# Which engine makes the weights' low parts while the first attention runs

## The chip, the cores and the metric

One core of one Trainium2 chip runs the whole program in one launch. The metric is the device time of an execution in microseconds (us), the median of several; lower is better. The names in the views: PE is TensorE's matrix unit (PEld its weight loads), DVE is VectorE, ACT is ScalarE, POOL is GpSimd, SP is SyncE, whose work here is to issue DMAs. L119 is line 119 of the kernel before; in the changed kernel every line from 1920 on stands one to three lines further down.

## The reference

One decoder layer on a sequence of 1024 tokens of width 1024. What matters here:

```python
h = rms_norm(x, norm1_g); proj = h @ w_in            # 54 column tiles of 128
p_rwkv, p_sb, q_mem, gate_logits = split(proj)
y_a = rwkv7_branch(p_rwkv, ...)                      # delta-rule recurrence, 8 heads x 64
y_b = stick_breaking_branch(p_sb, ...)               # "the first attention", 8 heads x 64
y_m = memory_branch(q_mem, mem, ...)                 # cross-attention into 256 memory tokens
x = x + (sum_b sigmoid(G_b) * (branch_b @ W_br[b])) @ W_out
x = x + conv_ffn(x)
```

Everything is float32.

## The kernel before

**How a product is made.** A float32 product goes to TensorE as three products of rounded operands: each operand is split into a high part (rounded to the format `fp32r`) and a low part (what the rounding left). For weights, `load_w` issues the DMA of a 128x1024 tile `wr` on SP's queue, `split_raw` lets ScalarE copy it to the high part `wh` (line 80) and another engine subtract to get the low part `wl = wr - wh` (line 81). Then `mm3` makes `wh.xhi`, `wh.xlo` and `wl.xhi` on TensorE (all matrix products are recorded under line 119, all transposes under line 105). `wr`, `wh` and `wl` have two buffers each, so the DMA of the next tile but one waits until both splitting engines have read the raw tile.

**How the work is ordered.** The program is written as a main stream with a filler. `run` builds `items`, a list of generators, each the projection of one weight tile (the heads' r, k, v: `shift_item`; the attention's values: `sb_v`; its q and k: `sb_qk`; branch gates: `gate_item`; the memory's keys and values: `mem_kv`). `stream` starts an item, that is, splits its weights, when the item before it begins its products, so a low part is made one item ahead of its first use. `weave` advances the main stream (with priority) and takes filler steps from `pump` between its steps. Main streams in turn: `rwkv_prep` for the four head pairs p = 0 to 3, then `sb_attn`, then `mem_attn` and the recurrence. During `sb_attn` the pump also steps through `inverse`, a chain of 62 pairs of VectorE instructions (lines 554 and 556) that inverts triangular blocks. A scheduler lays the instructions of each engine in one fixed order. An engine works through its own order and waits, at an instruction's place, for what that instruction needs.

**What the steps of the prediction touch.**
- In `rwkv_prep`: `chain(h)` (lines 464 to 474) builds two tiles per half on VectorE, among them `bk` by four instructions of line 472; `gram` (lines 476 to 494) multiplies them on TensorE and VectorE masks the result (line 486); lines 519 and 520 make a tile that ScalarE's line 522 must wait for, since it overwrites `g`, which line 520 reads; line 523 sends `g` to DRAM on ScalarE's queue, and a later `bk` takes over that buffer.
- In `differ` (lines 751 to 760): four tiles `A` are loaded by SP (line 756) and subtracted from on VectorE (line 757).
- In `sb_attn`: for each unit `front` makes logits on TensorE and their sigmoid on ScalarE (line 933), `weigh` runs a scan over them on VectorE (line 939), `mid` transposes the result on TensorE (line 105) and copies it back (line 951).
- POOL's other work in that stretch: small powers (lines 427, 781), a scaling (line 498) and DMAs (line 544).

Of the kernel before, what the change touches and what calls it, by code (L numbers as in the profile page):

```python
# [11 lines left out]
F32 = mybir.dt.float32  # L12
# [3 lines left out]
ALU = mybir.AluOpType  # L16
# [33 lines left out]
class Trunk:  # L50
# [27 lines left out]

    def split_raw(self, raw, hi, lo, fix=lambda ins: ins, fix_hi=None):
        (fix_hi or fix)(self.nc.scalar.activation(hi, raw, AF.Copy))  # L80
        fix(self.nc.gpsimd.tensor_tensor(lo, raw, hi.bitcast(F32), ALU.subtract))  # L81
        return hi, lo

    def split_w(self, src, fix=lambda ins: ins, fix_hi=None):
# [1821 lines left out]
    def run(self):  # L1906
        nc, tc = self.nc, self.tc
        self.setup()
        sx, sw, sl, sr = ExitStack(), ExitStack(), ExitStack(), ExitStack()
        self.pool_x = sx.enter_context(tc.tile_pool(name="xp", bufs=1))  # L1910
        self.pool_a = sr.enter_context(tc.tile_pool(name="ap", bufs=1, side="right"))
        self.bufs_w = {"w4": 3, "A": 4, "qk": 8, "at": 7, "ys": 1, "it": 1}
        self.pc = [self.pool_a.tile([128, NC], F32, name=f"pc{p}") for p in range(4)]
        self.inst = self.pool_a.tile([128, 64, 64], F32, name="inst", tag="inst")
        self.stored, self.open_gates = set(), []
        drain = lambda g: [None for _ in g]
        chain = itertools.chain
        self.pool_w = sw.enter_context(tc.tile_pool(name="w1", bufs=1, side="right"))
        krv, qk, mq = ([[] for _ in range(4)] for _ in range(3))
        krv[0].append(self.startup())  # L1920
        self.pin = True
        marks, self.fresh = {"k0"}, []
        self.marks = marks
        items = [self.shift_item(i + p, krv[p], f"{n}{p}") for p in range(4) for n, i in (("k", 4), ("r", 0), ("v", 8)) if (p, n) != (0, "k")]
        items += self.sb_v()
        self.v = []
        zero = self.t4("ys", n=512)
        nc.vector.memset(zero[0:1], 0.0)
        nc.sync.dma_start(self.vsd[0:1], zero[0:1])
        inv = self.inverse()  # L1930
        gq = [(b, d) for b in (1, 0) for d in range(8)]
        gq[14:14] = [(2, 0), (2, 1)]
        self.stored = set(gq)
        gate = lambda hook={}: self.gate_item(*gq.pop(0), hook)
        mark = lambda name: lambda: marks.add(name)
        for p in range(4):
            kp, kss, qp, early, hooks = self.sb_qk(p, qk[p])
            items += [*([self.differ] if p == 0 else []), kp, gate({**early, 6: self.spread_last} if p == 0 else early), kss, qp, gate(hooks), mark(f"sb{p}")]
        prep, mss, mv, mk = self.mem_kv()
        mqi = [None] * 4  # L1940
        for h in range(4):
            mqi[h] = self.mem_q(h, mq[h], {2: mqi[h - 1][1], 4: mark(f"mq{h - 1}")} if h > 1 else {})
        items += [gate({0: prep}), gate(), gate({2: prep}), lambda: mss(0), mv[0], lambda: mss(1), *mv[1:], *mk, mqi[0][0], mark("kv")]
        items += [self.mem_kss, gate({1: mqi[0][1]}), self.mem_kbc, mqi[1][0], mark("mq0")]
        items += [mqi[2][0], mqi[3][0], gate({2: mqi[3][1], 4: mark("mq3")}), gate(), mark("mem")]
        ld1, hk1, br1 = self.branch(1, True)
        ld2, hk2, br2 = self.branch(2, False)
        items += [lambda: drain(inv), gate(), ld1, gate(hk1), mark("y1"), *br1, ld2, gate(hk2), *br2, gate()]
        assert not gq
        pace = [0]  # L1950

        def pumped():
            due = 0
            for _ in self.stream(items):
                due += pace[0]
                while due >= 10:
                    due -= 10
                    next(inv, None)
                yield

        pump = pumped()

        def need(name):
            while name not in marks:
                next(pump)

        for p in range(4):
            self.weave(self.rwkv_prep(p, krv[p], need), pump, 1.0)
        pace[0] = 7
        need("sb0")  # L1970
        self.weave(self.sb_attn(qk, need), pump, 1.03, 0)
        need("kv")
        pace[0] = 8
        self.tight = True
        self.weave(self.mem_attn(mq, need), pump, 1.6, 0)
        self.tight = False
        need("mem")
        st2 = self.stage2()
        next(st2)
        need("y1")  # L1980
        self.weave(st2, pump, 2.15, 0)
        self.weave(self.group_norm(), pump, 1, 0)
        drain(pump)
        self.close_gates()
        self.pin = False
        sx.close()
        self.pool_l = sl.enter_context(tc.tile_pool(name="l4", bufs=16))
        self.branch_last()
        sums = self.out_proj()
        self.pool_a.tile([128, 56], F32, name="pad_a")  # L1990
        sw.close()
        self.bufs_r = {"u": 3, "p1": 2}
        self.pool_r = sr.enter_context(tc.tile_pool(name="ff", bufs=2, side="right", reuse_waits="tile"))
        self.up_phase(*sums)
        self.pool_r.tile([128, 40], F32, name="pad_r", bufs=1)
        self.down_phase()
        sr.close()
        sl.close()
# [67 lines left out]
```

## Time and profile before

| | |
|---|---|
| median of 3 runs | 1788.75 us (1787.13 to 1789.0) |
| the profiled execution's own time | 1788.76 us |
| its span (first to last instruction) | 1787.0 us, so 1.76 us lie around it |
| granted TensorE clock | 0.999 |
| busy share of the span: PE, DVE, ACT, POOL | 99%, 66%, 48%, 44% |
| low parts made under line 81 that the change moves | 41, on POOL 107.5 us |

How to read the views: a row of the timeline has start, duration, engine, line, operation, what it writes and reads, and in brackets how long its engine stood idle before it and who ended that. A group row has the count, then busy time and mean duration, then the idle time before. In a table by stages each engine has its busy time and, in brackets, its instructions. Matmuls overlap in the pipeline, so their rows' durations are longer than the distance between their starts.

### The profile page before, as it was taken

Reading aid. Unit: us, or ns where it says so; the run is one execution under the profiler, and the core shown is the slowest. Engines: PE = TensorE matmul, PEld = TensorE weight load, DVE = VectorE, ACT = ScalarE, POOL = GpSimd, SP = SyncE. Lnnn points to the kernel's source line nnn. Section 1 sums busy time; section 2 is a strip of 40 time slices with the busy share of each in tenths; the row PEclk is TensorE's granted clock in tenths of the full one; section 3 lists DMA queues with packets and bytes.
Section 4 is the critical chain, followed back from the end, with each engine's and each line's share of the span. In section 5 each row is a group of like instructions: output and inputs, shape, how many; then the busy total and the mean of one; then the engine's idle time right before and its main releaser. Section 6 shows DMA issues by size and latency. Waiting matters only on the chain.

```text
span 1787.0 us, 27327 instructions
## 1 busy us (share of the span) xinstructions
PE 1771.8 (99%) x10479; PEld 1440.1 (81%) x10479; DVE 1181.5 (66%) x1604; ACT 865.3 (48%) x1566; POOL 792.5 (44%) x448
## 2 busy tenths in 40 slices
PE   9999999999999999999999999999999999999999
PEld 7777778888888888777777888878888888888887
DVE  5667774898988624234443962687767777795597
ACT  6544343656666635534444334544444445454343
POOL 3223352331231453122332542487677677545454
PEclk9999999999999999999999999999999999999999
DMA  5145565111112443568554553223323323386476
GB/s 210 60 161 182 179 224 163 51 54 57 54 57 77 127 120 95 212 226 282 201 190 177 203 186 110 103 99 103 111 89 99 119 90 121 126 317 220 146 239 209
DMA packets 122771, 261.28 MB, mean 146 GB/s; under 512 B 28681, under 2 KB 43657, under 8 KB 122514
## 3 DMA queue, kind: packets, MB, share of 16 engines
q1 hardware_dynamic: 85026, 193.83, 32.9%
q10 hardware_dynamic: 33840, 53.10, 8.1%
q0 software_dynamic: 3776, 12.62, 2.4%
q8 instruction: 82, 1.34, 0.3%
q14 instruction: 47, 0.39, 0.1%
HBM read 178.99 MB, written 80.48 MB: 145 GB/s over the span
## 4 chain that ended last, share of the span: by engine, by line
PE 81%; DVE 6%; POOL 2%; issue 1%; ACT 1%; DMA 1%; DVEq 0%; SPq 0%; POOLq 0%; ACTq 0%
PE mm L119 66%; PE g L119 12%; PE g L105 3%; DVE it L554 1%; DVE at L939 1%; DVE inst L556 1%; DMA A<-yd 1%; POOL wl L1486 0%; DVE gall L1571 0%; DMA scr<-at 0%; POOL hf L781 0%; DVE w L344 0%; POOL l L1486 0%; DVE w L834 0%; DVE qk L877 0%
## 5 line engine op out<-in xcount | busy, mean ns | idle before, releaser
L81 POOL TENSOR_TENSOR wl<-wr,wh 128x1024 fp32r<-128x1024 f32 (+2 forms) x78 | 197.1, 2527 | 468.0 <-ACT wh L80 465.0
L119 PE MATMUL mm<-xhi,wh 128*128 128x512 f32 x784 | 260.3, 413 | 0.5 <-DVE w L331 0.4
L119 PE MATMUL mm<-xlo,wh 128*128 128x512 f32 x784 | 243.6, 392 | 0.0
L119 PE MATMUL mm<-xhi,wl 128*128 128x512 f32 x784 | 242.5, 391 | 0.0
L119 PEld LDWEIGHTS mm<-xlo,wh 128*128 128x128 f32 x784 | 147.1, 188 | 33.3 <-DVE xlo L208 0.4
L119 PEld LDWEIGHTS mm<-xhi,wl 128*128 128x128 f32 x784 | 147.0, 188 | 33.1 <-POOL wl L81 0.7
L119 PEld LDWEIGHTS mm<-xhi,wh 128*128 128x128 f32 x784 | 136.7, 190 | 28.9 <-issue 6.1
L80 ACT ACTIVATE wh<-wr 128x1024 fp32r<-128x1024 f32 (+2 forms) x78 | 81.8, 1049 | 130.9 <-PE mm L119 100.1
L119 PE MATMUL mm<-dw,da 128*128 128x512 f32 x528 | 120.3, 389 | 0.0
L119 PE MATMUL mm<-BT,l 128*128 128x512 f32 x504 | 118.0, 389 | 1.4 <-POOL l L1486 1.4
L1775 POOL TENSOR_TENSOR dw<-draw,dw 128x512 fp32r<-128x512 f32 x55 | 82.6, 1511 | 75.7 <-ACT dw L1773 70.0
L119 PEld LDWEIGHTS mm<-dw,da 128*128 128x128 f32 x528 | 99.1, 188 | 20.6
L119 PEld LDWEIGHTS mm<-BT,l 128*128 128x128 f32 x504 | 94.5, 188 | 21.5 <-POOL l L1486 1.8
L119 PE MATMUL mm<-BT,wh 128*128 128x512 f32 x352 | 108.7, 389 | 0.9 <-DVE BT L1396 0.9
L119 PE MATMUL mm<-B,wh 128*128 128x512 f32 x352 | 108.8, 390 | 0.0
L939 DVE TENSOR_TENSOR_SCAN at<-at,nrt 128x128 f32<-128x128 f32 (+3 forms) x64 | 96.3, 1514 | 18.2 <-ACT at L933 18.0
L1774 DVE TENSOR_TENSOR da<-draw,da 128x512 fp32r<-128x512 f32 x77 | 64.2, 839 | 51.5 <-ACT da L1772 51.2
L1486 POOL TENSOR_TENSOR l<-it,l 128x1024 fp32r<-128x1024 f32 x21 | 50.9, 2422 | 90.2 <-ACT l L1483 90.1
L119 PE MATMUL g<-dw,da 128*128 128x512 f32 x396 | 90.2, 389 | 0.0
L119 PEld LDWEIGHTS g<-dw,da 128*128 128x128 f32 x396 | 74.3, 188 | 15.4
L1772 ACT ACTIVATE da<-draw 128x512 fp32r<-128x512 f32 x77 | 48.2, 628 | 78.5 <-PE mm L119 32.0
L834 DVE TENSOR_TENSOR w<-w,nrt 128x1024 f32<-128x1024 f32 x24 | 46.6, 1941 | 57.3 <-ACT w L833 46.4
(337 smaller groups left out, 3979.2 us busy)
## 6 DMA issues: line engine op xcount, KB each, us to landing
wr<-in_w_in_dram SPq DMA_DIRECT2D x48, 512.0 KB, 3.6
draw<-actd SPq DMA_DIRECT2D x77, 256.0 KB, 2.9
draw<-in_w_down_dram SPq DMA_DIRECT2D x55, 256.0 KB, 4.6
at<-scr SPq DMA_DIRECT2D x24, 512.0 KB, 6.0
wr<-in_w_up_dram SPq DMA_DIRECT2D x22, 512.0 KB, 3.5
actd<-gall ACTq DMA_DIRECT2D x44, 256.0 KB, 3.2
rw<-in_w_up_dram SPq DMA_DIRECT2D x20, 512.0 KB, 3.5
gsd<-w ACTq DMA_DIRECT2D x18, 512.0 KB, 3.0
```

Of the source, the lines that this page charges most:

```text
L80: (fix_hi or fix)(self.nc.scalar.activation(hi, raw, AF.Copy))
L81: fix(self.nc.gpsimd.tensor_tensor(lo, raw, hi.bitcast(F32), ALU.subtract))
L105: self.pinned(self.nc.tensor.transpose(out, in_, self.ident[:n, :n]))
L119: self.pinned(self.nc.tensor.matmul(*a, **k))
L554: self.pinned(nc.vector.tensor_tensor(tv, X[:, 0:s, s : s + 1].to_broadcast([128, s, n]), X[:, s : s + 1, s + 1 : 64].to_broadcast([128, s ...
L556: self.pinned(nc.vector.tensor_tensor(X[:, 0:s, s + 1 : 64], X[:, 0:s, s + 1 : 64], tv, ALU.add))
L834: fix(nc.vector.tensor_tensor(g, g, self.nrb, ALU.mult))
L939: self.pinned(nc.vector.tensor_tensor_scan(sn[:, :W][:, ::-1], sn[:, :W][:, ::-1], self.nrt[:, 1152 - W :][:, ::-1], 1.0, ALU.mult, ALU.max))
L1486: ins = nc.gpsimd.tensor_tensor(lo, src, hi.bitcast(F32), ALU.subtract)
L1772: self.pinned(nc.scalar.activation(A[:, 0], a, AF.Copy))
L1774: self.pinned(nc.vector.tensor_tensor(A[:, 1], a, A[:, 0].bitcast(F32), ALU.subtract))
L1775: nc.gpsimd.tensor_tensor(Wt[:, 1], w, Wt[:, 0].bitcast(F32), ALU.subtract)
```

## The change

A field `low` of the class names the engine that runs line 81. It is POOL at the start, VectorE from the end of the first head pair's preparation, and POOL again from the end of the first attention.

```diff
     def split_raw(self, raw, hi, lo, fix=lambda ins: ins, fix_hi=None):
         (fix_hi or fix)(self.nc.scalar.activation(hi, raw, AF.Copy))
-        fix(self.nc.gpsimd.tensor_tensor(lo, raw, hi.bitcast(F32), ALU.subtract))
+        fix(self.low.tensor_tensor(lo, raw, hi.bitcast(F32), ALU.subtract))
         return hi, lo
...
         krv, qk, mq = ([[] for _ in range(4)] for _ in range(3))
+        self.low = nc.gpsimd
         krv[0].append(self.startup())
...
         for p in range(4):
             self.weave(self.rwkv_prep(p, krv[p], need), pump, 1.0)
+            self.low = nc.vector
         pace[0] = 7
         need("sb0")
         self.weave(self.sb_attn(qk, need), pump, 1.03, 0)
+        self.low = nc.gpsimd
```

41 instructions of line 81 leave POOL's order and stand in VectorE's: those for `wl_1015` to `wl_5640`. The orders of TensorE and ScalarE stay as they were. Three places in VectorE's order are of use later.

The first is in the fourth head pair's preparation, VectorE's order, as the difference between before (-) and now (+). `qk_2131` is the second half's other tile, `at_1752` the tile of lines 519 and 520, `wl_2031` and `wl_2077` are low parts of the attention's value weights:

```order
+L81 TENSOR_TENSOR wl_2031<-wr_2028,wh_2030 128x1024
 L519 TENSOR_TENSOR at_1752<-g_2046,at_1752 128x512
 L519 TENSOR_TENSOR at_1752<-g_2049,at_1752 128x512
-L467 SCALAR_TENSOR_TENSOR qk_2131<-qk_1867,at_1512 128x8x63
 L520 SCALAR_TENSOR_TENSOR at_1752<-at_1752,params,qk_1924 128x1024
-L468 TENSOR_SCALAR qk_2131<-at_1512 128x8
+L81 TENSOR_TENSOR wl_2077<-wr_2074,wh_2076 128x1024
 L757 TENSOR_TENSOR A_2278<-A_2278,w_314_1960 128x1024
 L486 TENSOR_TENSOR at_2086<-g_2087,kon 128x4x128
 L486 TENSOR_TENSOR at_2086<-g_2088,kon 128x4x128
+L757 TENSOR_TENSOR A_2281<-A_2281,w_319_1995 128x1024
 L486 TENSOR_TENSOR at_2108<-g_2109,kon 128x4x128
```

Two low parts come in; the rows of lines 467 and 468 taken out here now stand just ahead of `wl_2031`; and the second of the four `A` tiles (`A_2281`), which stood behind the second half's `bk`, now stands ahead of two masks of line 486 and of that `bk`. SP's order has its DMA ahead of the DMA of line 521 and of one weight tile, where it stood behind both.

The second place is the end of that preparation, VectorE's order again; `A_2284` and `A_2287` are the last two `A` tiles, `it_2311` is the first step of `inverse`:

```order
 L486 TENSOR_TENSOR at_2222<-g_2224,kon 128x4x128
 L757 TENSOR_TENSOR A_2284<-A_2284,at_2220 128x1024
+L81 TENSOR_TENSOR wl_2294<-wr_2291,wh_2293 128x1024
 L757 TENSOR_TENSOR A_2287<-A_2287,at_2252 128x1024
 L554 TENSOR_TENSOR it_2311<-inst 128x62
```

`wl_2294`, the low part for the first item after the values, stood in POOL's order behind a DMA; it now stands in VectorE's behind `A_2284`.

The third place is in the attention, VectorE's order as a difference; `it_4033` and `inst` belong to `inverse`, `at_4035` is a unit's scan, `w_682_4029` a branch gate:

```order
 L834 TENSOR_TENSOR w_682_4029<-w_682_4029,nrt 128x1024
 L554 TENSOR_TENSOR it_4033<-inst 128x972
+L81 TENSOR_TENSOR wl_4043<-wr_4040,wh_4042 128x1024
 L556 TENSOR_TENSOR inst<-inst,it_4033 128x36x27
 L939 SCALAR_TENSOR_TENSOR at_4035<-at_4035,nrt 128x128
```

Nothing but the low part comes in. The 1024-column scan of line 939 before it, which the prediction speaks of, stands three rows above this piece; `wl_3853`, the low part ahead of that scan, comes in twelve rows above the scan in the same way. SP's DMAs of weight tiles wait for VectorE's low part in this stretch where they waited for POOL's.

## The prediction

> **What bounds the kernel now.** I read the page first, then a table by stages over the stretch in which low parts move (125 to 640 us), then TensorE's waits in it, and last the timelines around each wait.
>
> ```profile
> PE 1771.8 (99%) x10479; PEld 1440.1 (81%) x10479; DVE 1181.5 (66%) x1604; ACT 865.3 (48%) x1566; POOL 792.5 (44%) x448
> sum 515.00, PE 511.50 PEld 419.20 DVE 388.42 ACT 278.73 POOL 168.50; mean PE 170.50 PEld 139.73 DVE 129.47 ACT 92.91 POOL 56.17
> PE g L105 <- DVE at L939: 1.8, 2, 1.6
> PE g L119 <- DVE qk L472: 1.2, 2, 1.0
> PE g L105 <- DVE at L336: 0.4, 1, 0.4
> ```
>
> TensorE works 99% of the span, and in the stretch it is idle for 515 - 511.5 = 3.5 us. All of its waits there, 1.8 + 1.2 + 0.4 = 3.4 us, end with VectorE. Neither TensorE's order nor its instructions change, so 3.5 us, 0.2% of the time, is about the most that the change can take away, whatever it frees elsewhere. What it can add has no such cap. A difference under 0.2% (3.6 us) is about what a measurement of this kernel cannot tell from no change.
>
> **The price of a moved instruction.** The groups of line 81 on POOL, and of the nearest VectorE operation:
>
> ```profile
> L81 POOL TENSOR_TENSOR wl<-wr,wh 128x1024 fp32r<-128x1024 f32 x41 | 107.5, 2621 | 205.4 <-ACT wh L80 205.3
> L877 DVE TENSOR_TENSOR qk<-w,qk 64x1024 fp32r<-64x1024 f32 x6 | 7.3, 1216 | 1.2 <-ACT qk L875 1.1
> ```
>
> VectorE has no row of this form. Line 877 is the same subtraction on the same types and row length, on half the partitions, and takes 1216 ns; POOL's own 2621 ns is the far end. I take 1.2 us, the row of the same engine: 41 x 1.2 = 49 us more work for VectorE (at the far end 107).
>
> But POOL's low parts already cost VectorE time. Two instructions of VectorE beside a low part on POOL, each followed by one of its form alone, and the last such case:
>
> ```profile
> 446.92 2.73 POOL L81 TENSOR_TENSOR wl<-wr,wh 128x1024 fp32r<-128x1024 f32 x1 [13.80 <-ACT wh L80]
> 447.42 3.27 DVE L554 TENSOR_TENSOR it<-inst 128x990 f32<-128x990 f32 x1
> 433.58 1.18 DVE L554 TENSOR_TENSOR it<-inst 128x990 f32<-128x990 f32 x1
> 136.66 2.85 DVE L466 TENSOR_TENSOR qk<-at,qk 128x512 f32<-128x512 f32 x1
> 189.25 0.69 DVE L466 TENSOR_TENSOR qk<-at,qk 128x512 f32<-128x512 f32 x1
> 612.21 2.42 DVE L554 TENSOR_TENSOR it<-inst 128x180 f32<-128x180 f32 x1
> ```
>
> POOL's low part ends at 446.92 + 2.73 = 449.65, and the instruction that began beside it ends at 450.69, one time of its own (1.18) later: it stood for 2.1 us. Each VectorE row that ran beside a moved low part, set against the shortest row of its form, gives 34 rows longer by over 0.15 us, the first at 136.66 and the last at 612.21, by 62 us in all. So VectorE pays 49 us and gets 62 back: its busy time in the stretch falls by about 13 us (ends: 13 us less; 107 us more, if none comes back at the far price).
>
> **Where a low part is later.** POOL made each one nearly as soon as its high part was there. VectorE makes it when its order comes to it. For `wl_4043`, in the attention:
>
> ```profile
> 463.85 2.51 POOL L81 TENSOR_TENSOR wl<-wr,wh 128x1024 fp32r<-128x1024 f32 x1 [5.27 <-ACT wh L80]
> 472.08 1.17 DVE L554 TENSOR_TENSOR it<-inst 128x972 f32<-128x972 f32 x1
> 483.03 0.62 PE L119 MATMUL mm<-xhi,wl 128*128 128x512 f32 x2
> ```
>
> Its place is behind the second row, which ends at 473.25, so it ends near 474.5, 8 us later than on POOL; TensorE's first use is at 483.0, because an item's weights are split an item ahead. That cover, 8.5 us here, hides the delay at no cost; gone, the 8 us would be TensorE's. The next DMA into the tile's buffer waits for the low part too, and is due only two items on. Put beside their first use in this way, the other places in the attention have 6 us or more, those before it less; the two thinnest follow below.
>
> **The wait at 468 us: 1.6 us go.**
>
> ```profile
> 464.03 4.47 DVE L939 TENSOR_TENSOR_SCAN at<-at,nrt 128x1024 f32<-128x1024 f32 x1
> 423.60 2.29 DVE L939 TENSOR_TENSOR_SCAN at<-at,nrt 128x1024 f32<-128x1024 f32 x1 [1.53 <-ACT at L933]
> 468.65 1.06 PE L105 MATMUL g<-kon,at 128*128 128x128 f32 x8 [1.57 <-DVE at L939]
> ```
>
> The scan met the low part of 463.85 and took 4.47 us where another of its form took 2.29; TensorE stood 1.57 us. With the low part behind the scan, it ends by 464.0 + 2.3 = 466.3, and TensorE is free for it at 468.65 - 1.57 = 467.1. Ahead of it `wl_3853` adds 1.2 us, and the hold at 447.42 gives back 2.1. I take -1.6 (ends: 0 and -1.6; the other 0.2 of this row and the 0.4 at line 336, another -0.6, I leave for the lower end).
>
> **The wait at 263 us: 1.2 us go.**
>
> ```profile
> 242.70 2.35 DVE L468 TENSOR_SCALAR qk<-at 128x8 f32<-128x8 f32 x1
> 244.96 2.80 DVE L472 TENSOR_TENSOR qk<-qk,qk 64x512 f32<-64x512 f32 x4
> 248.32 0.39 PE L119 MATMUL mm<-wl,xhi 128*128 128x512 f32 x1
> 250.19 3.40 DVE L520 SCALAR_TENSOR_TENSOR at<-at,params,qk 128x1024 f32<-128x1024 f32 x1
> 253.52 0.16 DVE L468 TENSOR_SCALAR qk<-at 128x8 f32<-128x8 f32 x1
> 254.81 0.34 ACTq L523 DMA_DIRECT2D ggd<-qk  x1
> 261.19 2.81 DVE L472 TENSOR_TENSOR qk<-qk,qk 64x512 f32<-64x512 f32 x4 [3.39 <-DMA ggd<-qk]
> 263.43 0.46 PE L119 MATMUL g<-qk,qk 64*128 64x128 f32 x2 [0.96 <-DVE qk L472]
> 264.14 1.01 PE L119 MATMUL g<-qk,qk 64*128 64x128 f32 x13 [0.26 <-DVE qk L472]
> ```
>
> A chain: line 520 was held by a low part on POOL, ScalarE's line 522 waited for it, its DMA left at 254.81, landed when VectorE's `bk` began at 261.19, and TensorE stood 0.96 + 0.26 = 1.2 us. Now the tiny line 468 at 242.70 takes the 0.16 us that it takes at 253.52. `bk` of the first half then ends at 242.9 + 2.8 = 245.7; lines 467 and 468, moved up, add 0.7; `wl_2031` ends at 247.6, 0.7 us ahead of its first use at 248.32 (ends: no cost, or 1.4 us if `bk` cannot begin before 244.96). Lines 519 and 520 add 2.5: 250.1, which is 3.5 us sooner than 253.59, and the DMA with it, so `bk` can begin at 257.7. Is VectorE there? Behind line 520 stand `wl_2077`, `A_2278` and two masks (3.6 us, 253.7), then the moved `A_2281`. Its DMA is now behind a weight tile's, which waits for `wl_2031`:
>
> ```profile
> 246.10 0.67 SPq L76 DMA_DIRECT2D wr<-in_w_v_dram  x1
> 254.52 0.67 SPq L756 DMA_DIRECT2D A<-vsd  x1
> DMA to landing us min/median/max: 5.2/6.6/7.5
> ```
>
> It leaves at about 247.6 + 0.7 = 248.3 instead of 254.52 and lands, as the four `A` tiles did, 5.2 to 7.5 us later: 253.5 to 255.8. Subtraction, two masks and line 466 (1.2 + 1.2 + 0.6) bring VectorE to `bk` at 256.7 to 258.8, its 2.8 us end by 261.6, and TensorE is free for it at 263.43 - 0.96 = 262.5. Cover 0.9 us. I take -1.2 (ends: -1.2, and +3 by the third rival).
>
> **The wait that comes in, at 285 us: 1.0 us.**
>
> ```profile
> 276.07 4.04 SPq L756 DMA_DIRECT2D A<-vsd  x2
> 283.59 1.34 DVE L757 TENSOR_TENSOR A<-A,at 128x1024 f32<-128x1024 f32 x1 [14.31 <-DMA A<-vsd]
> 284.83 0.62 PE L119 MATMUL mm<-xhi,wl 128*128 128x512 f32 x2
> ```
>
> VectorE stands 14.31 us for the DMA of `A_2284`; before, that held up nothing that TensorE needed soon. Now `wl_2294` is queued behind it: 283.59 + 1.3 + 1.2 = 286.1, and TensorE needs it at 284.83, 1.3 us sooner. That DMA goes out when the values that TensorE makes have been stored, so when TensorE gains 1.2 us at 263, both ends shift together. With its landing at the median of 6.6 in place of 276.07 to 283.59 = 7.5 us, 0.4 is left. I take +1.0 (ends: 0 and +1.3), nearer to the row of this very DMA.
>
> **The sum.** From the profiled execution's own 1788.76 us, which is the median of the runs (1788.75): -1.6 - 1.2 + 1.0 = -1.8, so 1787.0 us. Its own range is 1786.0 (nothing new at 285) to 1788.4 (1.4 late at 248). After 640 us nothing is moved, and TensorE's later work follows it.
>
> **The rivals.**
>
> *VectorE becomes the bound: slower.* Its slices in the attention are full:
>
> ```profile
> 380.00:400.00 20.00, 20.00 (x147) 17.11 (x145) 19.73 (x15) 12.76 (x25) 8.47 (x3) 1.00 0.15 44
> 400.00:420.00 20.00, 20.00 (x150) 16.56 (x149) 19.90 (x17) 10.75 (x21) 2.41 (x1) 1.00 0.17 60
> 440.00:460.00 20.00, 20.00 (x146) 16.56 (x144) 19.80 (x17) 15.96 (x28) 7.32 (x3) 1.00 0.14 40
> 460.00:480.00 20.00, 18.43 (x132) 15.53 (x130) 19.83 (x16) 9.30 (x18) 2.51 (x1) 1.00 0.09 27
> ```
>
> Each gets one low part. If nothing comes back, they need 79.26 + 4 x 1.2 = 84.1 of their 80 us, so the scans of line 939 reach TensorE up to 4.1 us later; both waits stay, and the one at 285 comes in: +5.1, 1793.9 us. It decides at the scan at 464: whether it takes 2.3 us or still 4.5. Against it speak the 34 held rows. The Trainium skill (Perfetto Trace Analysis, Optimizing Scalar/DVE Operations) says that work of a saturated VectorE may sensibly go to other engines, even GpSimd, which is the reverse of this change; by that rule the time would come out here. The same section warns that the two share a port into SBUF, so that moving work between them might not help; the held rows side with the warning. Chance 0.11.
>
> *All of TensorE's waits on VectorE go and none comes in.* Then -3.4: 1785.4 us; with the rest of the idle 3.5, 1785.2. For it: VectorE gets 13 us lighter, SP's queue ahead of the `A` tiles moves up too. Against it: the DMA at 276.07 waits for TensorE's own values. Chance 0.19.
>
> *The moved `A_2281` lands late.* If its DMA still leaves near 254.5 and lands at 261.9, `bk` ends 1.2 + 1.2 + 0.6 + 2.8 later, 267.7 instead of 264.0: TensorE loses 3.7 there in place of gaining 1.2, with -1.6 and +1.0 it is +3.1, 1791.9 us. For it: in that stretch many DMAs are under way. Against it: nothing in its new place waits past 248. Chance 0.07.
>
> *The time is only passed on.* TensorE gets ahead and stands the same 2.8 us at its next need of another engine, the sigmoids of line 933 say, as VectorE did before its scan at 423.60 (1.53 us). Then 0, 1788.8 us. Chance 0.15. That the change does not do what it says is ruled out by the order: 41 of line 81 stand in VectorE's.
>
> **How the numbers follow.** The forecast's case has what is left, 0.48. The range from 1785.0 to 1791.9 leaves out the slower rival and a little beyond the cap of 3.5 us. Faster by over 0.2% is below 1785.2: a part of the second rival, 0.13. Slower by over 0.2% is above 1792.3: the first rival and the tail of the third, 0.13. Within it: 0.74.
>
> **What would show it.** Right: in the profile after, VectorE's busy time from 125 to 640 us near 375 (388.42 - 13) with low parts of 1.2 us each; the scan at 464 at 2.3 us and no wait of TensorE behind it; `bk` near 258 and no wait at 263; a wait of about 1 us for a low part near 284. Wrong: VectorE's busy time at 430 or more, low parts of over 2 us, waits of TensorE on line 939 in the attention, or any wait of TensorE on a low part other than the one at 284, which would mean that a place in VectorE's order comes later than I read it.

## The result and the profile after

| | before | after |
|---|---|---|
| median (lowest to highest) of 19 runs each | 1788.23 us (1786.24 to 1790.78) | 1784.27 us (1783.01 to 1785.68) |
| ratio of after to before, 95% interval | | 0.9979 (0.9973 to 0.9985) |
| the profiled execution's own time; its span | 1788.76 us; 1787.0 us | 1783.84 us; 1782.1 us |

The changed kernel is 1788.23 - 1784.27 = 4.0 us faster, 0.21%. The forecast was 1787.0 us with a range from 1785.0: the direction was right, the gain larger than the range allowed.

The engines' line of the page; the row of the stretch from 125 to 640 us in the table by stages (PE, PEld, DVE, ACT and POOL in this order, then the granted clock, the DMA engines' busy share and their GB/s); all of TensorE's waits in that stretch (us in total, times, the longest); and the moved instructions by line, with duration in ns (least, median, most):

```profile
PE 1767.9 (99%) x10479; PEld 1438.4 (81%) x10479; DVE 1169.8 (66%) x1645; ACT 864.9 (49%) x1566; POOL 685.4 (38%) x407
```
```profile
125.00:640.00 515.00, 513.88 (x3467) 422.12 (x3466) 378.40 (x415) 279.07 (x477) 66.33 (x34) 1.00 0.35 111
```
```profile
PE mm L119 <- DVE wl L81: 0.8, 1, 0.8
PE g L105 <- DVE at L336: 0.4, 1, 0.4
```
```profile
L81 DVE TENSOR_TENSOR wl<-wr,wh x41: 1198/1219/2227, 114.9 to 621.1; 128x1024 fp32r<-128x1024 f32 x41
```

VectorE has 41 instructions more than before and is busy for less: 378.40 us in the stretch, where it was 388.42. A moved low part takes 1.22 us (median of 41). The waits on lines 939 and 472 are gone, and one for a low part has come in.

**Where the 4 us lie.** TensorE runs the same 10479 products in the same order in both traces, so the k-th product of one is the k-th of the other, and the difference of their starts tells at each place how far the changed kernel is ahead. A jump in that difference is time won or lost there:

| place (us, before) | what TensorE waited for | jump | foretold |
|---|---|---|---|
| up to 12 (the program's start) | nothing that the change touches | -0.35 | 0 |
| 205 | not shown; transposes of line 105 | -0.35 | 0 |
| 248 | a low part, `wl_2031`; a new wait | +1.00 | 0 (ends 0 and +1.4) |
| 263 to 269 | `bk` | -1.71 | -1.2 |
| 285 | a low part, `wl_2294` | 0 | +1.0 |
| 329 | a scan of line 939 | -0.39 | 0 |
| 468 | a scan of line 939 | -1.83 | -1.6 |
| 600 | not shown; logits of line 119 | -0.48 | 0 |
| sum to 640 | | -4.11 | -1.8 |

From 640 us to the end the two profiled executions differ by another 0.8 us: -1.4 at 1207 (the slow spell in the last section) and +0.7 at 832. Neither goes with the change: at 832 the other eight runs differ from the kernel before by -0.15 to +1.0 us, and by nothing in e1, e6 and e7.

**The scan at 464 (before).** VectorE after, and TensorE behind it:

```profile
460.65 2.28 DVE L939 TENSOR_TENSOR_SCAN at<-at,nrt 128x1024 f32<-128x1024 f32 x1
...
467.59 1.22 DVE L81 TENSOR_TENSOR wl<-wr,wh 128x1024 fp32r<-128x1024 f32 x1
```
```profile
464.78 0.40 PE L119 MATMUL g<-qk,qk 128*128 128x256 f32 x2
465.02 1.03 PE L105 MATMUL g<-kon,at 128*128 128x128 f32 x8
```

The scan takes 2.28 us in place of 4.47, the low part comes 4.7 us behind it, and TensorE's row has no bracket: no wait.

**The places at 248 and 263.** VectorE after; then TensorE around the new wait, and POOL's only instruction there:

```profile
241.97 0.17 DVE L468 TENSOR_SCALAR qk<-at 128x8 f32<-128x8 f32 x1
242.04 2.78 DVE L472 TENSOR_TENSOR qk<-qk,qk 64x512 f32<-64x512 f32 x4
...
245.46 1.87 DVE L468 TENSOR_SCALAR qk<-at 128x8 f32<-128x8 f32 x1
247.24 1.21 DVE L81 TENSOR_TENSOR wl<-wr,wh 128x1024 fp32r<-128x1024 f32 x1
...
249.69 1.28 DVE L520 SCALAR_TENSOR_TENSOR at<-at,params,qk 128x1024 f32<-128x1024 f32 x1
...
254.87 1.23 DVE L757 TENSOR_TENSOR A<-A,w 128x1024 f32<-128x1024 f32 x1 [0.43 <-DMA A<-vsd]
...
259.02 2.81 DVE L472 TENSOR_TENSOR qk<-qk,qk 64x512 f32<-64x512 f32 x4 [1.13 <-DMA ggd<-qk]
```
```profile
247.37 0.39 PE L119 MATMUL mm<-wh,xlo 128*128 128x512 f32 x1
248.51 0.50 PE L119 MATMUL mm<-wl,xhi 128*128 128x512 f32 x1 [0.75 <-DVE wl L81]
...
262.72 1.16 PE L119 MATMUL g<-qk,qk 64*128 64x128 f32 x16
```
```profile
244.99 2.30 POOL L498 TENSOR_TENSOR it<-qk,pc 128x1024 f32<-128x1024 f32 x1 [12.64 <-DVE qk L472]
```

The first tiny line 468 is down from 2.35 to 0.17 us and line 520 from 3.40 to 1.28, as foretold. The second line 468, moved up ahead of `wl_2031`, takes 1.87 us: it stands beside POOL's scaling of line 498, which starts when the first half's `bk` (line 472) is done, and so sooner than before (244.99 against 247.83). It ends at 245.46 + 1.87 = 247.33, where POOL's row ends at 247.29. `wl_2031` is late by that, and TensorE stands 0.75 us for it. At 263 there is no wait left.

**The place at 285.** SP's own waits and the store of the values on ScalarE's queue, each before and then after; then SP's queue and VectorE after:

```profile
SPq L756 <- DMA vsd<-at: 3.2, 2, 2.8
SPq L756 <- DMA vsd<-at: 3.8, 2, 2.6
```
```profile
270.32 0.37 ACTq L743 DMA_DIRECT2D vsd<-at  x1
268.91 0.37 ACTq L743 DMA_DIRECT2D vsd<-at  x1
```
```profile
273.81 3.40 SPq L756 DMA_DIRECT2D A<-vsd  x2
```
```profile
279.51 1.23 DVE L757 TENSOR_TENSOR A<-A,at 128x1024 f32<-128x1024 f32 x1 [11.20 <-DMA A<-vsd]
280.66 1.22 DVE L81 TENSOR_TENSOR wl<-wr,wh 128x1024 fp32r<-128x1024 f32 x1
```

In both kernels SP waits for this store to land before it sends the DMA of `A_2284`. The store leaves 270.32 - 268.91 = 1.4 us sooner, and the DMA follows it after 273.81 - 268.91 = 4.9 us instead of 276.07 - 270.32 = 5.75. So the DMA leaves 276.07 - 273.81 = 2.3 us sooner than before, and it takes 279.51 - 273.81 = 5.7 us instead of 7.5. `wl_2294` is done at 281.9, before TensorE uses it at 283.4.

### The profile page after: what moved, and what is told of

It is laid out like the page before. It is cut to its first block, busy times and chain, and to the rows that moved or that the text cites. A ratio compares the mean times of both kernels' runs of the same rounds, so it can differ in the third digit from the quotient of the medians.

```text
span 1782.1 us, 27312 instructions
## 1 busy us (share of the span) xinstructions
PE 1767.9 (99%) x10479; PEld 1438.4 (81%) x10479; DVE 1169.8 (66%) x1645; ACT 864.9 (49%) x1566; POOL 685.4 (38%) x407
## 4 chain that ended last, share of the span: by engine, by line
PE 91%; DVE 3%; issue 2%; POOL 2%; DMA 1%; ACT 1%; SPq 0%; ACTq 0%; DVEq 0%; POOLq 0%
PE mm L119 73%; PE g L119 14%; PE g L105 4%; DMA A<-yd 1%; DVE qk L217 0%; POOL wl L1486 0%; DVE gall L1571 0%; DMA at<-in_xT_dram 0%; DMA x<-in_x_dram 0%; ACT xhi L207 0%; DMA vd<-qk 0%; POOL inv L427 0%; ACT qk L212 0%; POOL it L1505 0%; DVE g L1553 0%
## 5 line engine op out<-in xcount | busy, mean ns | idle before, releaser
L81 POOL TENSOR_TENSOR wl<-wr,wh 128x1024 fp32r<-128x1024 f32 (+2 forms) x37 | 89.6, 2420 | 289.5 <-ACT wh L80 289.5
L939 DVE TENSOR_TENSOR_SCAN at<-at,nrt 128x128 f32<-128x128 f32 (+3 forms) x64 | 86.3, 1353 | 30.8 <-ACT at L933 30.4
L779 POOL TENSOR_TENSOR hn<-hn,eps 128x16 f32<-128x16 f32 (+1 forms) x12 | 8.5, 705 | 221.3 <-ACT hn L778 221.3
```

What stands on the lines that cost most here:

```text
L81: fix(self.low.tensor_tensor(lo, raw, hi.bitcast(F32), ALU.subtract))
L779: nc.gpsimd.tensor_tensor(v3(t), v3(t), self.eps.unsqueeze(2).to_broadcast([128, 8, nh]), ALU.add)
L939: self.pinned(nc.vector.tensor_tensor_scan(sn[:, :W][:, ::-1], sn[:, :W][:, ::-1], self.nrt[:, 1152 - W :][:, ::-1], 1.0, ALU.mult, ALU.max))
```

## The experiments

The theory: a POOL instruction that reads tiles holds a VectorE instruction that reads tiles too, for most of POOL's duration; the change takes 41 such POOL instructions away, and the time falls where the held instruction was the one that TensorE waited for. The rivals: the gain is made by the other order of VectorE's and SP's instructions in the fourth pair's preparation (A); the time comes from outside the stretch, and the two lie together by chance (B); VectorE as a whole is lighter and so ahead of time, and no single low part matters (C); it is POOL's time and queue that come free, not its reads (D).

### One stage alone: the attention, the preparations

`e1_attn_only` moves the low parts in the attention only, `e2_prep_only` those of the second to fourth pair's preparation only.

```diff
         for p in range(4):
             self.weave(self.rwkv_prep(p, krv[p], need), pump, 1.0)
-            self.low = nc.vector              # e1
...
+        self.low = nc.vector                  # e1
+        self.low = nc.gpsimd                  # e2
         self.weave(self.sb_attn(qk, need), pump, 1.03, 0)
```

> Low parts go to VectorE only from the start of the first attention, the 14 of the head pairs' preparation stay on POOL. Theory (a low part on POOL holds VectorE's next instruction that reads two tiles, and three such holds reached TensorE): the wait at 468 us goes (-1.8 us), the small ones at 329 and 600 go (-0.4 each), the one at 263 (1.2 us) stays, and the new wait at 248 is absent: 2.6 us under the kernel before, about 1785.6. Rival A (the gain is made by the other order of VectorE's and SP's instructions in the fourth head pair's preparation, A and line 467 moved up): nothing of it is left, 1788.2. Rival B (it lies outside the stretch, in the start and at 1210 us): 1787 or so, with both waits still there.

> Low parts go to VectorE only in the preparation of head pairs 2 to 4 and return to POOL at the start of the first attention. Theory: the wait at 263 goes (1.6 us by the distance of starts), the new one of 0.8 at 248 is there, the wait at 468 stays: about 0.8 us under the kernel before, 1787.4. Rival A (order in the preparation): the whole 4 us, 1784.3. Rival B (outside the stretch): 1787, with the wait at 263 still there.

Measured: e1 1785.63 us against 1787.86 on the same chip, ratio 0.999 (0.9982 to 0.9999); e2 1787.04 us, 0.9996 (0.9987 to 1.0005), which by time alone is not told from no change. TensorE's waits in the stretch, of e1 and then of e2:

```profile
PE g L119 <- DVE qk L472: 0.8, 2, 0.5
```
```profile
PE g L105 <- DVE at L939: 1.8, 2, 1.6
PE mm L119 <- DVE wl L81: 0.7, 1, 0.7
```

Beside these each has the 0.4 at line 336. By starts, e1 wins 1.82 at 468, 0.42 at 329 and 0.49 at 600; e2 wins 0.28 at 205 and 1.75 at 263 and loses 0.99 at 248. Each stage's waits go with its own low parts, but for one: e1 also wins 0.47 at 263, where its `bk` has one of its waits shortened; why was not followed. The gains of the two medians, 2.23 and 0.82 us, come to 3.05 us together; the 4.0 of the whole change is within what their intervals (some 1.5 us either way) allow. VectorE's busy time in the stretch is 375.81 us in e1 and 389.78 in e2: the lightening is the attention's; in the preparations VectorE pays 1.4 us more than it gets back.

### One low part alone, and all but that one

`e3_one_at_464` moves only `wl_4043`, the low part beside the scan at 464; `e4_all_but_464` is the changed kernel with that one left on POOL. The number is the program's count of tiles at that place.

```diff
-        fix(self.nc.gpsimd.tensor_tensor(lo, raw, hi.bitcast(F32), ALU.subtract))
+        fix((self.nc.vector if self.uid in (688,) else self.nc.gpsimd).tensor_tensor(lo, raw, hi.bitcast(F32), ALU.subtract))
```

> Only one low part, the one that POOL made at 463.85 us, goes to VectorE; the other 40 stay on POOL. Theory: the scan at 464 takes 2.3 us in place of 4.5 and the wait of TensorE behind it shrinks or goes: 1.8 us under the kernel before at most, 1786.4; the low parts ahead of it still hold VectorE, so its scan may begin as late as before, which leaves TensorE free of it by 0.8 us. Rival A (order): 1788.2 with the wait still there. Rival C (VectorE was late at 468 by the sum of all holds ahead, so that one does little): the wait stays at 1 us or more, 1787.5 or above.

> The changed kernel with that one low part back on POOL. Theory: the scan meets it again, or another instruction of VectorE does, since VectorE runs 3 us earlier there than before; if it is the scan, 1.0 to 1.8 us of TensorE's wait return (1785.3 to 1786.1); if it is one behind the scan, nothing returns (1784.3). Rival C (the sum of holds ahead): nothing returns, whichever instruction is held, as VectorE is by then early enough.

Measured: e3 1786.11 us, 0.9991 (0.9982 to 0.9999); e4 1785.22 us, 0.9981 (0.9973 to 0.999). The scan in e3, in e2 (whose low part there is still on POOL), and VectorE and POOL in e4:

```profile
464.30 2.29 DVE L939 TENSOR_TENSOR_SCAN at<-at,nrt 128x1024 f32<-128x1024 f32 x1
```
```profile
462.75 4.48 DVE L939 TENSOR_TENSOR_SCAN at<-at,nrt 128x1024 f32<-128x1024 f32 x1
```
```profile
460.97 2.29 DVE L939 TENSOR_TENSOR_SCAN at<-at,nrt 128x1024 f32<-128x1024 f32 x1
463.29 3.24 DVE L896 SCALAR_TENSOR_TENSOR qk<-w,offs,qk 64x1024 fp32r<-64x1024 f32 x1
...
462.21 3.23 POOL L81 TENSOR_TENSOR wl<-wr,wh 128x1024 fp32r<-128x1024 f32 x1 [5.07 <-ACT wh L80]
```

In e3 one instruction of 27 thousand has changed its engine, the scan is short, and TensorE's wait there falls from 1.57 to 0.2 us; by starts 1.76 us are won, all of it at this place, and the median falls by 1.75. So a single low part matters, and C does not hold for this wait. In e4 the place was not hurt: there the scan was already running when POOL came, and it was POOL that took longer (3.23 us where it takes 2.4 alone), and line 896 behind the scan that was held (3.24 us, 1.28 alone). Here, which of two colliding instructions begins first decides which is held. e4 alone could not have told theory from C; e3 does.

### POOL reads, POOL writes

Both add work to the changed kernel behind the first 33 moved low parts, into a raw tile that nobody reads again: `e5_pool_reads` lets POOL do the subtraction once more, `e6_pool_writes` lets it fill the tile with zeros twice. The outputs' computation is untouched.

```diff
+        if self.low is self.nc.vector and self.uid < 900:
+            self.nc.gpsimd.tensor_tensor(raw, raw, hi.bitcast(F32), ALU.subtract)   # e5
...
+            for _ in range(2):
+                self.nc.gpsimd.memset(raw, 0.0)                                     # e6
```

> The changed kernel, and behind each of the first 33 moved low parts POOL repeats the subtraction into the raw tile, which nobody reads any more: work added, the output is not touched. POOL is then as busy as before the change and reads two tiles each time. Theory (what counts is that POOL's subtraction holds VectorE's next instruction of two tiles): 33 holds of up to 2.1 us come back, now behind the low part: VectorE's busy time from 125 to 640 us goes from 378 to 425 to 445 us, it is full in the attention, and TensorE waits for its scans again: 1787 to 1793. Rival D (what counts is that POOL's own queue is free, or that the low part takes 1.2 us in place of 2.6): VectorE's busy time within 5 us of 378, the time at 1784.3, or later only where POOL's small jobs stand behind the added ones.

> The same, but POOL fills the raw tile with zeros, twice, in place of the subtraction: POOL's queue is taken at the same places and the raw tile is released as late, but POOL reads nothing. The output is not touched. Theory, if it is POOL's reading that holds VectorE: busy time of VectorE within 10 us of 378 and the time within 1 us of the changed kernel's, 1784.3. If any POOL instruction on the tiles holds it: as the run with the subtraction, by POOL's time in the fills. Rival D (POOL's queue): as the run with the subtraction.

Measured, against 1787.94 us of before on that chip: e5 1798.13 us, ratio 1.0058 (1.0046 to 1.007); e6 1788.42 us, 0.9997 (0.9989 to 1.0006). Lines behind the added ones have numbers two higher in e5 and three higher in e6. The stretch, the added group, TensorE's two longest waits and one scan of e5 (L941 is line 939):

```profile
125.00:640.00 515.00, 505.82 (x3365) 413.11 (x3364) 423.90 (x410) 275.68 (x470) 154.50 (x62) 1.00 0.34 110
```
```profile
L83 POOL TENSOR_TENSOR wr<-wr,wh 128x1024 f32<-128x1024 f32 x32 | 93.9, 2934 | 224.1 <-DVE wl L81 151.2 <-issue 36.8 <-DVE w L331 14.3
```
```profile
PE g L107 <- DVE at L941: 3.9, 3, 1.8
PE mm L121 <- DVE wl L81: 2.0, 2, 1.6
```
```profile
331.88 2.58 DVE L941 TENSOR_TENSOR_SCAN at<-at,nrt 128x128 f32<-128x128 f32 x1
```

The same of e6, the stretch, the added group and its longest wait:

```profile
125.00:640.00 515.00, 511.12 (x3421) 419.60 (x3420) 374.50 (x412) 277.62 (x474) 123.07 (x95) 1.00 0.35 110
```
```profile
L84 POOL MEMSET wr<- 128x1024 f32 x64 | 61.6, 962 | 234.4 <-DVE wl L81 167.0 <-ACT at L954 21.7 <-issue 20.5
```
```profile
PE mm L122 <- DVE wl L81: 3.5, 2, 3.1
```

With the reads VectorE's busy time is 423.90 - 378.40 = 45.5 us longer for the same instructions, 1.4 us for each of the 32 reads of 2.93 us; a scan that takes 0.42 us alone takes 2.58; and TensorE waits for scans again. With 64 fills of 0.96 us VectorE is no slower than in the changed kernel (374.50). So POOL's reading holds VectorE, and neither its time nor its queue does. The Trainium skill (SBUF — State Buffer, section "Who interferes with whom") says this: a VectorE instruction with two inputs from SBUF contends with a GpSimd instruction that reads it, not with one that only writes, and whoever issues first keeps the shared pair for its whole instruction; e5, e6 and the pair of rows in e4 agree. Line 468, which reads one tile only, was held too (last section).

Two things were not as the theory had them. e5's median is beyond the upper end that it gave (1793): the profiled execution took 1794.0 us, which is the 10.2 us by starts over the changed kernel's (1.9 of them at 285, where TensorE waits for `wl_2294`), but the six lay between 1794.0 and 1802.57, and what the others lost beyond that no profile shows. And e6 is 4 us slower than the changed kernel. In the profiled execution all of it is lost at one place; the eleven runs lie between 1784.44 and 1789.92, so it may not come in every execution (SP's queue; then VectorE; then TensorE; then two slices by stages, where the figure ahead of the last two is the granted clock):

```profile
271.69 0.84 SPq L76 DMA_DIRECT2D wr<-in_w_in_dram  x1
273.01 4.12 SPq L759 DMA_DIRECT2D A<-vsd  x2
```
```profile
284.07 1.23 DVE L760 TENSOR_TENSOR A<-A,at 128x1024 f32<-128x1024 f32 x1 [13.78 <-ACT w L858]
285.21 1.22 DVE L81 TENSOR_TENSOR wl<-wr,wh 128x1024 fp32r<-128x1024 f32 x1
```
```profile
286.49 1.22 PE L122 MATMUL mm<-xhi,wl 128*128 128x512 f32 x2 [3.14 <-DVE wl L81]
```
```profile
284.00:286.00 2.00, 0.00 (x0) 0.00 (x0) 1.93 (x2) 1.12 (x2) 0.00 (x0) 1.00 0.19 70
286.00:288.00 2.00, 1.51 (x4) 1.22 (x5) 1.93 (x5) 0.00 (x0) 1.44 (x2) 0.51 0.02 4
```

It is the wait that the forecast had put at 285: `wl_2294` behind `A_2284` (here line 760), whose DMA now has a weight tile's (line 76) just ahead of it on SP's queue and takes 284.07 - 273.01 = 11.1 us until VectorE begins. The bracket names ScalarE's line 858, which ended at that moment; in the changed kernel VectorE's row (279.51) ran ahead of that line's (855 there, 283.21), so what is left to wait for is the DMA. TensorE stands 3.14 us, and its granted clock is 0.51 in the slice in which it goes on; by starts 3.3 us are lost up to the first product behind the wait and 1.5 us over the next ones. Why the DMA took so long is open: e5 has a weight tile's just ahead of it too, and there it took 7.6 us, as before the change (7.5). So e6's time says nothing for or against the theory; VectorE's busy time does.

### The new wait at 248, taken away in two ways

`e7_one_back_at_248` puts `wl_2031` alone back on POOL; `e8_scaling_too` gives VectorE the scaling of line 498 as well, while it makes the low parts, so that POOL reads nothing there.

```diff
-        fix(self.low.tensor_tensor(lo, raw, hi.bitcast(F32), ALU.subtract))
+        fix((self.nc.gpsimd if self.uid in (326,) else self.low).tensor_tensor(lo, raw, hi.bitcast(F32), ALU.subtract))   # e7
...
-            self.ordered(nc.gpsimd.tensor_tensor(
+            self.ordered(self.low.tensor_tensor(                                                                              # e8
```

> The changed kernel with the one low part that TensorE waited for at 248 us back on POOL; VectorE's order goes back with it, line 467 behind line 519. Theory: the wait of 0.8 us at 248 goes, but POOL's low part holds the tiny line 468 at 242 for 2.2 us again, so line 520 ends about 0.7 us later than in the changed kernel and 0 to 0.7 us of the wait at 263 return: 0.1 to 0.8 us under the changed kernel, 1783.5 to 1784.2. If the wait at 263 was shortened by the order of lines 467 and 468: it is back at 1.2 us, 1784.7 or more.

> The changed kernel with POOL's scaling of line 498 on VectorE too in head pairs 2 to 4: six instructions of 1.2 us more for VectorE, and POOL keeps only small jobs. Theory: line 468 at 245 us is not held for 1.7 us by the scaling, the low part of 248 is there before TensorE needs it, -0.8; line 520 comes 1.2 us for the scaling and 1.2 for the low part now ahead of it later, less 1.7: bk may be up to 0.7 late: 1783.5 to 1784.2. Rival (VectorE in the preparation has no room for it): TensorE's waits in 125 to 300 us grow by over 1 us, 1785.3 or more.

Measured, against 1787.94: e7 1783.72 us, ratio 0.9973 (0.9963 to 0.9984); e8 1783.2 us, 0.9977 (0.9968 to 0.9987), a little under the range expected of it. VectorE and TensorE in e8:

```profile
245.67 0.17 DVE L468 TENSOR_SCALAR qk<-at 128x8 f32<-128x8 f32 x1
245.75 1.22 DVE L81 TENSOR_TENSOR wl<-wr,wh 128x1024 fp32r<-128x1024 f32 x1
```
```profile
247.81 0.39 PE L119 MATMUL mm<-wl,xhi 128*128 128x512 f32 x1
```

With the scaling off POOL, line 468 takes 0.17 us and the low part is there 247.81 - 246.97 = 0.8 us before its use: this shows that POOL's scaling had held it. By starts both kernels are ahead of the changed one by 0.9 us at 248 (0.91 and 0.92) and by nothing else of 0.15 us or more in the stretch; only the 0.4 at line 336 is left of TensorE's waits. Both beat the kernel before; that they beat the changed one is shown at this place of the trace, but not by the medians, whose intervals overlap.

A does not hold at 468: e1 and e3 leave the preparation's low parts on POOL and win there all the same. In e7 lines 467 and 468 stand again where they stood before the change, and the wait at 263 does not come back. What the moved `A_2281` does there was not tried alone.

B is left to answer. In e2, e3, e7 and e8 every jump of 0.2 us or more in the stretch lies at a place whose POOL instructions were changed, in e1 every one but the 0.47, and the medians follow their sums: e1 -3.2 by starts and -2.2 measured, e2 -1.0 and -0.8, e3 -1.8 and -1.8, each within its interval (e1's at its edge). Beyond 640 us there are jumps of up to 1.5 us (at 832, 1151 and 1207), but they come and go between the runs and follow no change. So the gain comes from the stretch.

## Why the prediction was right and wrong

**Right: the mechanism.** POOL's low parts held VectorE, a low part on VectorE costs 1.2 us (1.22 measured), VectorE gets lighter by taking the work over (378.40; foretold about 375), the scan at 464 falls to 2.3 us (2.28), and the chain of line 520, its DMA and `bk` moves up. `bk` began at 259.0, where 257.7 to 258.8 was worked out; the covers there held, with `A_2281` landing at 254.9. `wl_4043` came 4.7 us behind the scan and nobody waited for it. The first rival (VectorE the bound) is out by its own test at the scan. That the time is only passed on is out too: the 1.76 us that e3 wins at 468 are still there at 640.

**Wrong, and it put the time outside the range: the cap.** "3.5 us, 0.2% of the time, is about the most that the change can take away" was read from TensorE's idle time. Leaving out the program's start and the new wait at 248, the stretch won 4.11 - 0.35 + 1.00 = 4.8 us. A 512-column product's row is 0.39 us long, but the next one starts 0.23 us later when nothing is missing:

```profile
247.14 0.39 PE L119 MATMUL mm<-wh,xhi 128*128 128x512 f32 x1
```

Here the next row, shown above, starts at 247.37. An idle time counted from such a row's end therefore leaves out 0.39 - 0.23 = 0.16 us of the wait, and a wait under 0.16 us does not show at all. The Trainium skill (Perfetto Trace Analysis, Tensor Engine Instruction) says that the profiler works out such an end and does not measure it. At 468 the row ahead of TensorE's wait, and at 329 the row behind one, both before:

```profile
466.67 0.40 PE L119 MATMUL g<-qk,qk 128*128 128x256 f32 x2
...
329.26 0.33 PE L105 MATMUL g<-kon,at 128*128 128x128 f32 x1 [0.18 <-DVE at L939]
```

The start of 468.65 is 1.98 us behind that of 466.67; after, 465.02 is 0.24 behind 464.78. That is 1.74 us where the bracket said 1.57 (and 0.08 more by the next product). At 329 the bracket says 0.18 and 0.39 was won; at 205 and 600 no bracket stood at all, and 0.35 and 0.48 were won (at 600 the row's end leaves 0.15 us of idle time, for which the timeline prints none). Of the sum, -1.6 was -1.83; -1.2, which was two waits, was -1.71; and three places that had no term of their own won 0.35 + 0.39 + 0.48 = 1.2 (the 0.2 at 329 had been left "for the lower end"; the 0.4 at line 336 stayed).

**Wrong: the wait at 285, +1.0.** What failed is the landing times. The prediction let "both ends shift together", and the store of the values did leave with TensorE, 1.4 us sooner. But the store landed 0.85 us faster (4.9 for 5.75) and the DMA of `A_2284` behind it 1.8 us faster (5.7 for 7.5), 2.65 us in all, where `wl_2294` had been worked out as 1.3 us late. The term was sized by "the row of this very DMA"; the median landing that it weighed, 6.6 us, was itself more than the 5.7 that came. In the ten profiled executions that DMA took from 4.5 us (e8) to 11.1 (e6), so one row could not size it; what sets its time is open. That the place is thin was right: the same wait is there in e5 (1.6 us) and e6 (3.14 us).

**Wrong in its value, inside its ends: the place at 248.** Taken at 0 with ends 0 and +1.4, it cost +1.00. The step that failed is that line 468, "moved up", would add 0.16 us in its new place: POOL's other reader, the scaling of line 498, was not asked about. It waits for `bk`, so the gain at `bk` pulled it onto the moved instruction. A wait on a low part other than the one at 284 is the sign of being wrong that the prediction itself had named.

The two errors, +1.0 that did not come and +1.00 that did, cancel, which is luck. What is left is 1787.0 - 1784.3 = 2.7 us. Of it 0.23 + 0.51 + 1.22 = 2.0 are waits that the cap undercounted. Another 0.5 is where the forecast started: 1788.76, the median of three runs, where that of 19 is 1788.23. The remaining 0.2 is less than the interval leaves open.

## What to carry to other kernels

Before moving work from VectorE to POOL, or leaving it there, look for VectorE rows that are longer than the shortest of their form, and set POOL's rows beside them: 1.2 us on VectorE was cheaper here than 2.6 us on POOL, though VectorE was full. When a POOL instruction goes, ask of every one that stays when it will now start, and what it will meet there. Size a wait of TensorE by the distance between starts of the two products around it, against their distance where nothing is missing, and not by the idle time that the profile shows.

## What the runs showed that was not expected

**A slow spell after a short pause.** At 1200 us, far from the change, TensorE stands 2.2 to 2.3 us for line 1618 in every kernel. Behind it, before and after:

```profile
1207.30 4.32 PE L119 MATMUL mm<-B,l 128*128 128x512 f32 x12 [2.23 <-DVE u L1618]
1208.00:1212.00 4.00, 4.00 (x12) 3.10 (x12) 2.77 (x4) 2.88 (x5) 4.00 (x3) 0.58 0.09 11
```
```profile
1203.84 2.99 PE L119 MATMUL mm<-B,l 128*128 128x512 f32 x12 [2.30 <-DVE u L1618]
1204.00:1208.00 4.00, 4.00 (x18) 3.08 (x18) 3.15 (x5) 3.31 (x5) 4.00 (x3) 1.00 0.08 27
```

The same twelve products take 4.32 us at a granted clock of 0.58 or 2.99 us at 1.00. Of the ten profiled executions five were slow here, with 4.30 to 4.58 us (before, e1, e4, e6, e7), and five quick, with 2.99 or 3.00 (after, e2, e3, e5, e8): it goes by the execution and not by the change. The Trainium skill (TensorE: Matmul & The Clock Gate, "What's actually happening") has the clock set by windows that run freely, and so by where in one a pause falls; the scatter agrees, though a pause of 2.2 us is shorter than the idle window of about 3.4 us that it gives.

**A tiny instruction can be held like a large one.** Line 468 reads one tile of 8 columns and takes 0.16 us alone; beside POOL's readers it took 2.35 us (before) and 1.87 us (after), until POOL's row ended.
